# A hybrid decoder step on one core: feed-forward input in a fixed order, cache rows and stores on another queue

## The chip, the cores and the metric

The kernel runs on one core of a Trainium2 chip. The time is device microseconds of one execution, the median of three runs. The engines are named as in the profile: PE (TensorE) with PEld, its weight loads, DVE (VectorE), ACT (ScalarE), POOL (GpSimd) and SP (SyncE). Transfers are issued by SP, POOL and ACT and carried by the core's 16 DMA engines.

## What is computed

One layer of a hybrid causal decoder for 256 prompt tokens and 8 x 4 sample tokens, which share all weights (model width 2048, feed-forward width 5632, everything in float32):

```python
h = _rms_norm(x, g_pre_mix)
(qa, ka, va, za, ba, aa, qb, kb, vb, uc, ga, gb, gc) = _split(h @ w_in, IN_SPLITS)
# A: gated DeltaNet on qa, ka, va -> out_a
# B: dilated sliding-window attention on qb, kb, vb, with the cached windows for the sample tokens -> out_b
# C: multi-scale pooling of uc -> oc
merged = (jax.nn.sigmoid(ga) * (out_a @ w_br_a)
          + jax.nn.sigmoid(gb) * (out_b @ w_br_b)
          + jax.nn.sigmoid(gc) * (oc @ w_br_c))
x = x + _rms_norm(merged @ w_out, g_post_mix)
gate, up = _split(_rms_norm(x, g_pre_ffn) @ w_gu, (D_FF, D_FF))
x = x + _rms_norm((jax.nn.silu(gate) * up) @ w_down, g_post_ffn)
```

Besides the new x, the states are returned: the windows of keys and values (win1, win2, win3), moved on by the new tokens, the DeltaNet state, and the last rows of convolution and pool.

## The kernel before

The 288 tokens are the columns of every activation tile (128 x 288); a weight tile is 256 x 512 values (512 KB) and yields 24 matmuls. Each product is made of three matmuls: weights and activations are split into a rounded part and a rest (wh, wl; xgh, xgl), and wh x xh, wh x xl and wl x xh are added up in PSUM. So each weight tile passes through `feed` (lines 172 to 185): SP loads it into one of five `raw` buffers, ACT casts it to wh (line 180), DVE subtracts to get wl (line 184). Three wh and three wl buffers let this run ahead of PE.

`run_items` goes through a planned list of products. Beside it run generators (`start`, `step`): after every weight tile, each of them emits so many steps as its rate says. The program is not executed in the order in which it is written: a planner puts the instructions of each engine in an order by their simulated times, except where `behind` or `chain` ties one instruction to another. Each engine and each queue then takes its instructions strictly in that order.

**The sample tokens' attention.** `evac_qkv` (line 955 on) copies the new q, k and v out of PSUM, turns them and stores them on POOL's queue (`self.dq`): to the scratch tensor `scr`, and as the newest rows of the output windows (lines 986, 988, 991). `attn_sample` (line 1077 on) is a generator at 4.4 steps a tile. It reads the cached keys, then the cached values, in rows of 128 x 512 values (256 KB) into five buffers `kr` (KR = 5). Of groups 1 and 2 there are 32 + 16 rows for keys and as many for values, loaded on line 1106 from a view whose outermost size is 4 (`src[m, kv][:4]`, then 32 rows of 512 values); of group 0 there are 8 + 8, line 1111, from a view of 128 rows. Rows of the new tokens come from `scr` (lines 1089, 1112). Four rows are fetched ahead (`KR - 1`). Each row of groups 1 and 2 feeds four DVE instructions (lines 1142 for keys, 1192 for values). These are tied to each other and, by `paced`, to the newest wl. The cache copies of line 165 (win_sample<-cache_win) are issued by SP later, from about the middle of the kernel on.

**From the mixer to the feed-forward.** `evac_out` evacuates merged @ w_out block by block: ACT squares it, DVE adds the squares to `nacc`, ACT scales it by g_post_mix into `tt`. After the last block `post_mix` makes one more wh and wl (`feed(3)`) and takes the root of the mean square: `rms_rows` sums over the partitions with small PE matmuls, ACT takes the root, DVE the reciprocal, and PE spreads it over the partitions (rmsb, line 368). `ffn_input` then makes, for each of 16 blocks d, the product of t with rmsb (line 1367), the new x (line 1368), and from it xgh on ACT (line 373) and xgl on DVE (line 374). The first item of the feed-forward is a wide one of 12 tiles that takes the blocks as they come. `ffn_norm` squares the new x and adds the squares up to r2, which the evacuations of the first blocks need (`evac_ffn_gate`).

**The tail.** After the last product `down_done` adds identity x xr into PSUM for the first blocks of kind 'e' in the string TAIL (the x products, line 1433), makes the last `rms_rows`, multiplies every y by it (line 1440) and adds x: 'e' on PE with a copy by ACT, 'q' on POOL, 'v' on DVE (line 1449).

Of the kernel before, what the change touches and what calls it, by code (L numbers as in the profile page):

```python
# [21 lines left out]
TS = 6  # L22
TAIL = 'eveqqqeeeqqqevqe'
PCB = 3
KR = 5
# [63 lines left out]
class Layer:  # L89
# [3 lines left out]
    def __init__(self, ctx, tc, a, o):  # L93
        self.ctx, self.tc, self.nc, self.a, self.o = ctx, tc, tc.nc, a, o
        P = self.pool
        self.cp = P("cp")
        self.raw_p = P("rawp", 5)
        self.wh_p = P("whp", 3)
        self.wl_p = P("wlp", 3)
        self.up = P("up")  # L100
        self.sm = P("sm", 2)
        self.dr = P("dr", space=DRAM)
        self.pm = P("pm", 4, space=PSUM)
        self.pb = P("pb", 4, space=PSUM)
        self.ufree = deque(range(NU))
        self.uslot = {}
        self.bg = []
        self.chained = {}
        self.tiles = deque()
        self.pend = deque()  # L110
        self.items = []
        self.n = 0
        self.paced_to = None
        self.raws = deque()
        self.hold = None
        self.out_a, self.out_b, self.out_c = {}, {}, {}
        self.dq = self.nc.gpsimd
# [54 lines left out]
    def feed(self, ahead):  # L172
        nc = self.nc
        while len(self.pend) < ahead and (self.raws or self.tiles):
            if not self.raws:
                self.load()
            raw = self.raws.popleft()
            wh = self.wh_p.tile([128, 2, 512], F32R, name="wh")
            wl = self.wl_p.tile([128, 2, 512], F32R, name="wl")
            i = nc.scalar.copy(wh, raw)  # L180
            if self.hold is not None:
                self.behind(i, self.hold)
                self.hold = None
            self.last_wl = nc.vector.tensor_tensor(wl, raw, wh.bitcast(F32), op=OP.subtract)  # L184
            self.pend.append((wh, wl))

# [81 lines left out]
    def chain(self, ins, key="sample"):  # L268

        if key in self.chained:  # L270
            self.behind(ins, self.chained[key])
        self.chained[key] = ins

    def paced(self, ins):
# [80 lines left out]
    def rms_rows(self, *accs):  # L355

        nc, st = self.nc, (0, 128, 160)
        p = self.ps("rms")
        for k, acc in enumerate(accs):
            for i, t in enumerate(st):  # L360
                nc.tensor.matmul(p[:, i:i + 1], lhsT=acc[:, t:t + 128], rhs=self.c["ones"][:, 0:1],
                                 start=k == i == 0, stop=k == len(accs) - 1, skip_group_check=True)
        r = self.small(3, "rs")
# [129 lines left out]
    def mixer_plan(self):  # L493
# [53 lines left out]
        for br, off, name, nk in (("a", 9744, "w_br_a", 4), ("c", 13840, "w_br_c", 4), ("b", 11792, "w_br_b", 2)):  # L547
# [8 lines left out]
            for n in range(4):  # L556
                if br == "a" or (br == "c" and n):
# [5 lines left out]
                          after=(lambda br=br: self.branch_done(br)) if n == 3 else None)  # L563
        self.tt, self.xr = {}, {}
        for n in range(4):
# [4 lines left out]
        for part, gs in enumerate(((0, 1, 2), (3, 4, 5), (6, 7, 8), (9, 10))):  # L570
            for f in gs:
                if f == 0:
                    gate, up = self.evac_ffn_gate(0), self.evac_ffn_up(0)
                    self.plan_wide(wg, 8, 0, DFF, lambda: self.xg,
                                   lambda b, ps, gate=gate, up=up: gate(b, ps) if b < 4 else up(b - 4, ps),
                                   ready=lambda t: self.ffn_input(min(16, (t // 3) * 4 + (2, 4, 6)[t % 3])))
                    self.plan_half(wg, 8, DFF + 256, lambda: self.xg, lambda b, ps, up=up: up(b + 2, ps))
                    continue
# [376 lines left out]
    def evac_qkv(self, kind, g):  # L955
        vT = []

        def evac(h, ps):
# [10 lines left out]
            for tb in ([2] if kind == 0 else [1, 2] if (kind == 1 and g == 0) else [0, 1, 2]):  # L969
# [5 lines left out]
                for hp in range(2):  # L975
# [6 lines left out]
                    if tb < 2:  # L982
                        if not (g == 0 and tb == 0):
                            o = self.o[f"win{g + 1}_prompt"][0, 0].rearrange("r k h d -> r k (h d)")
                            r0 = 0 if g == 0 else tb * 128
                            self.dq.dma_start(o[r0:r0 + 128, kind - 1, cs], n[:, :256])
                    else:
                        self.dq.dma_start(self.scr[kind, g][:, cs], n[:NS, :256])
                        if kind > 0:
                            o = self.o[f"win{g + 1}_sample"][0].rearrange("b r k h d -> b r k (h d)")  # L990
                            self.dq.dma_start(o[:, WIN[g] - 4:, kind - 1, cs], n[:NS, :256])
                    if kind == 2 and tb < 2:
# [84 lines left out]
    def attn_sample(self, pool):  # L1077
# [8 lines left out]
        def by_t(dst, kind, g):  # L1086
            src = scr[kind, g].rearrange("(b t) d -> t b d", t=4)
            for t in range(4):
                dq.dma_start(dst[t * 32:t * 32 + 32], src[t][:, None, :].to_broadcast([8, 4, 512]))

# [3 lines left out]
        for t in range(4):  # L1094
            dq.dma_start(big[:, t], q0s[t][:, None, :].to_broadcast([8, 16, 512]))
        cw = [a["cache_win1"][0], a["cache_win2"][0], a["cache_win3"][0]]
# [4 lines left out]
        def sources(kv):  # L1101

            for g, dil, n in ((1, 4, 32), (2, 16, 16)):
                src = cw[g].rearrange("b (q m r) k h d -> m k r (b q) (h d)", q=4, r=dil)
                for m in range(n):
                    yield g, (m if g == 1 else 32 + m), lambda kr, s=src[m, kv][:4]: dq.dma_start(kr, s)  # L1106
            for g in (1, 2):
                yield g, 47 + g, lambda kr, g=g: by_t(kr, 1 + kv, g)
            src = cw[0].rearrange("b (s m) k h d -> m k (b s) (h d)", m=8)
            for m in range(8):  # L1110
                yield 0, m, lambda kr, s=src[m, kv]: dq.dma_start(kr, s)
            yield 0, 8, lambda kr: dq.dma_start(kr, scr[1 + kv, 0][:, None, :].to_broadcast([32, 4, 512]))

# [17 lines left out]

        for _ in range(KR - 1):
            load()
# [204 lines left out]
    def evac_out(self, n):  # L1338
        def evac(b, ps):
# [6 lines left out]
            if k == 9:  # L1346
                self.warm_sqrt(self.nacc)
            t = self.U(name="t")
            nc.scalar.activation(t, ps, AF.Copy, scale=self.p["g_post_mix"][:, k:k + 1])
            self.tt[k] = t  # L1350
        return evac

    def post_mix(self):
        nc = self.nc
        for pr in self.mg.values():
            self.free(*pr)
        self.feed(3)
        self.rmix = self.rms_rows(self.nacc, self.last)
        self.free(self.last)
        self.xg = []  # L1360
        self.ffn_rms = self.start(self.ffn_norm(self.nacc), 1.6)

    def ffn_input(self, n):
        nc = self.nc
        for d in range(len(self.xg), n):
            t, x = self.tt[d], self.xr[d]
            nc.vector.tensor_tensor(t, t, self.rmix, op=OP.mult)
            nc.vector.tensor_tensor(x, x, t, op=OP.add)
            self.xg.append(self.scaled_split(x, self.p["g_pre_ffn"][:, d:d + 1], "xg"))
            self.free(t)  # L1370

    def ffn_norm(self, acc):
        nc = self.nc
        for d in range(16):
            while len(self.xg) <= d:
                yield
            self.sq_add(acc, self.xr[d], d == 0)
            yield
        self.r2 = self.U(name="r2")
        nc.scalar.copy(self.r2, self.rms_rows(acc))  # L1380
        self.free(acc)


    def evac_ffn_gate(self, f):
# [19 lines left out]
    def evac_down(self, part, n):  # L1404
        def evac(b, ps):
# [6 lines left out]
            if part == 3:  # L1412
# [5 lines left out]
                if k == 9:  # L1418
                    self.warm_sqrt(self.nacc)
                nc.scalar.activation(self.y[k], self.y[k], AF.Copy, scale=self.p["g_post_ffn"][:, k:k + 1])  # L1420
        return evac

    def down_done(self, blks, part):
# [3 lines left out]
        if part < 3:  # L1427
            return
        kind = dict(zip(range(16), TAIL))
        pre = {}  # L1430
        for d in [d for d in range(16) if kind[d] == "e"][:TPRE]:
            pre[d] = self.add_bank(len(pre))
            nc.tensor.matmul(pre[d][:, :NT], lhsT=self.c["ident"], rhs=self.xr[d], start=True, stop=False)
        r = self.rms_rows(self.nacc, self.last)
        pool = self.pool("yo", 6)
# [85 lines left out]
```

## Time and profile before

| | us |
|---|---|
| median of 3 runs (2057.72 to 2062.92) | 2061.14 |
| the profiled execution | 2068.37 |
| its span | 2066.6 |
| PE busy in it | 2010.6 |
| mean granted clock | 0.992 |

A row of a table of stages has: its bounds in us from the start, its length; busy us and instructions of PE, PEld, DVE, ACT and POOL; the granted clock; the mean busy share of the 16 DMA engines (over 1 where packets of several queues overlap); and GB/s. A row of a list of transfers has the output and input, the issuing queue, the count, KB each and the median us from issue to landing. A row of DMA queues has packets, MB and the share of the 16 engines' time. A timeline row has start and length in us, engine, line, output<-input, shape, a count where rows in a series were merged, and in brackets the idle time before it with what ended it. A row of waits has the waiting engine with its line, what it waited for, us in total, times, and the longest in us.

### The profile page before, as it was taken

How to read it: one execution, taken by the hardware profiler on the slowest of the kernel's cores; microseconds unless marked ns; L12 is line 12 of the kernel's file. 1: busy time of each engine (PE TensorE's matmuls, PEld its weight loads, DVE VectorE, ACT ScalarE, POOL GpSimd, SP SyncE). 2: the span in 40 equal slices, each digit the busy share in tenths (PEclk: the TensorE clock that was granted, in tenths of full speed). 3: DMA queues.
4: the chain of work that ended last, by engine and by line, in shares of the span. 5: the costliest groups of instructions: out<-in, count | busy, mean ns of one | idle time of the engine just before them, and what ended most of it. 6: DMA issues, size and time to landing. Idle time of an engine off the chain costs nothing. (4 is left out here: it accounts for less than half of the span.)

```text
span 2066.6 us, 38707 instructions
## 1 busy us (share of the span) xinstructions
PE 2010.6 (97%) x15212; PEld 1984.4 (96%) x15212; DVE 1324.2 (64%) x2857; ACT 893.8 (43%) x1414; POOL 291.6 (14%) x504
## 2 busy tenths in 40 slices
PE   8999999999799999989999989999999999999998
PEld 8989998999799999989999989999999999999997
DVE  7969558567688779878875475543554445454555
ACT  6654473453344444333334454334333333333344
POOL 2326312523320022322000000000000000000001
PEclk9999999999999999999999989999999999999999
DMA  8565546959995668998677646766767767677662
GB/s 268 160 182 169 176 140 197 228 173 238 219 205 183 181 184 198 226 220 245 195 229 234 218 160 212 226 222 217 225 216 228 230 217 226 218 225 227 217 205 97
DMA packets 240310, 425.50 MB, mean 206 GB/s; under 512 B 42736, under 2 KB 83200, under 8 KB 238464
## 3 DMA queue, kind: packets, MB, share of 16 engines
q1 hardware_dynamic: 207712, 384.72, 63.1%
q0 software_dynamic: 32272, 37.73, 8.0%
q8 instruction: 119, 1.95, 0.4%
q10 hardware_dynamic: 144, 0.59, 0.1%
q14 instruction: 63, 0.52, 0.1%
HBM read 410.44 MB, written 66.63 MB: 231 GB/s over the span
## 5 line engine op out<-in xcount | busy, mean ns | idle before, releaser
L184 DVE TENSOR_TENSOR wl<-raw,wh 128x1024 fp32r<-128x1024 f32 x585 | 720.2, 1232 | 519.0 <-ACT wh L180 516.7
L180 ACT CAST wh<-raw 128x1024 fp32r<-128x1024 f32 x585 | 612.7, 1050 | 917.9 <-PE m L254 792.3
L253 PE MATMUL m<-hh,wh 128*128 128x288 f32 x1792 | 532.7, 299 | 4.2 <-ACT wh L180 3.7
L255 PE MATMUL m<-hh,wl 128*128 128x288 f32 x1792 | 524.0, 298 | 8.3 <-DVE wl L184 8.3
L254 PE MATMUL m<-hl,wh 128*128 128x288 f32 x1792 | 531.3, 298 | 0.0
L253 PE MATMUL m<-xgh,wh 128*128 128x288 f32 x1408 | 415.8, 297 | 4.0 <-ACT xgh L373 4.0
L254 PE MATMUL m<-xgl,wh 128*128 128x288 f32 x1408 | 415.8, 296 | 3.2 <-DVE xgl L374 3.2
L255 PE MATMUL m<-xgh,wl 128*128 128x288 f32 x1408 | 414.6, 296 | 0.0
L255 PEld LDWEIGHTS m<-hh,wl 128*128 128x128 f32 x1792 | 335.1, 189 | 13.1 <-DVE wl L184 10.7
L253 PEld LDWEIGHTS m<-hh,wh 128*128 128x128 f32 x1792 | 337.7, 189 | 7.8 <-ACT wh L180 4.2
L254 PEld LDWEIGHTS m<-hl,wh 128*128 128x128 f32 x1792 | 338.2, 189 | 1.9 <-issue 1.8
L253 PEld LDWEIGHTS m<-xgh,wh 128*128 128x128 f32 x1408 | 265.5, 189 | 4.6 <-ACT xgh L373 4.3
L254 PEld LDWEIGHTS m<-xgl,wh 128*128 128x128 f32 x1408 | 266.4, 189 | 3.6 <-DVE xgl L374 3.5
L255 PEld LDWEIGHTS m<-xgh,wl 128*128 128x128 f32 x1408 | 265.4, 189 | 0.0
L253 PE MATMUL m<-hidh,wh 128*128 128x288 f32 x704 | 207.5, 295 | 0.0
L254 PE MATMUL m<-hidl,wh 128*128 128x288 f32 x704 | 207.2, 295 | 0.0
L255 PE MATMUL m<-hidh,wl 128*128 128x288 f32 x704 | 206.5, 295 | 0.0
L1449 POOL TENSOR_TENSOR yo<-y,xr 128x288 f32<-128x288 f32 x7 | 5.6, 821 | 1060.7 <-DVE y L1440 1060.7
L254 PEld LDWEIGHTS m<-hidl,wh 128*128 128x128 f32 x704 | 132.4, 188 | 0.0
L253 PEld LDWEIGHTS m<-hidh,wh 128*128 128x128 f32 x704 | 132.2, 188 | 0.0
L255 PEld LDWEIGHTS m<-hidh,wl 128*128 128x128 f32 x704 | 131.9, 188 | 0.0
L1106 POOL DMA_DIRECT2D kr<-cache_win x96 | 65.4, 682 | 250.0 <-DVE junk L1142 136.9
(386 smaller groups left out, 2704.4 us busy)
## 6 DMA issues: line engine op xcount, KB each, us to landing
raw<-w_in SPq DMA_DIRECT2D x247, 512.0 KB, 4.5
raw<-w_gu SPq DMA_DIRECT2D x176, 512.0 KB, 4.0
raw<-w_down SPq DMA_DIRECT2D x88, 512.0 KB, 4.9
win_sample<-cache_win SPq DMA_DIRECT2D x64, 512.0 KB, 5.4
kr<-cache_win POOLq DMA_DIRECT2D x112, 256.0 KB, 10.7
raw<-w_out SPq DMA_DIRECT2D x32, 512.0 KB, 5.0
win_sample<-cache_win SPq DMA_DIRECT2D x32, 508.0 KB, 5.2
st<-state_gdn SPq DMA_DIRECT2D x64, 128.0 KB, 3.2
```

The source lines that it names most:

```text
L180: i = nc.scalar.copy(wh, raw)
L184: self.last_wl = nc.vector.tensor_tensor(wl, raw, wh.bitcast(F32), op=OP.subtract)
L253: nc.tensor.matmul(out, lhsT=wh[:, c], rhs=xh, start=k == 0, stop=False)
L254: nc.tensor.matmul(out, lhsT=wh[:, c], rhs=xl, start=False, stop=False)
L255: nc.tensor.matmul(out, lhsT=wl[:, c], rhs=xh, start=False, stop=k == nk - 1)
L1106: yield g, (m if g == 1 else 32 + m), lambda kr, s=src[m, kv][:4]: dq.dma_start(kr, s)
L1449: (nc.vector if how == "v" else nc.gpsimd).tensor_tensor(out[:, d % 2], y, x, op=OP.add)
```

## The change

- In `evac_qkv` and `attn_sample`, the stores of the new rows, the loads from `scr` and all loads of cache rows are issued by SP instead of POOL, and three rows instead of four are fetched ahead (`KR - 2`).
- `ffn_input` ties product, sum and rest into one DVE chain: for the blocks of one call first product and sum of each, then the rests. The first wl after it is tied behind its last sum (`hold_wl`). `post_mix` no longer feeds. The squares in `ffn_norm` are added behind the newest wl, at 1.1 steps a tile instead of 1.6.
- The first feed-forward blocks are copied out of PSUM as they are; product with r2, SiLU and split follow in the generator `ffn_first`.
- The scaling of the last four blocks, of t and of y, comes after the last square.
- `rms_rows` is cut into `rms_sums` and `rms_bcast`; in the tail the x products are tied behind the sums. Two blocks of kind 'v' become 'e'.

```diff
-TAIL = 'eveqqqeeeqqqevqe'
+TAIL = 'eeeqqqeeeqqqeeqe'
...
             self.last_wl = nc.vector.tensor_tensor(wl, raw, wh.bitcast(F32), op=OP.subtract)
+            if self.hold_wl is not None:
+                self.behind(self.last_wl, self.hold_wl)
+                self.hold_wl = None
...
     def rms_rows(self, *accs):
 
+        return self.rms_bcast(self.rms_sums(*accs)[0])
+
+    def rms_sums(self, *accs):
...
+        return p, m
+
+    def rms_bcast(self, p):
+        nc, st = self.nc, (0, 128, 160)
...
                 if f == 0:
-                    gate, up = self.evac_ffn_gate(0), self.evac_ffn_up(0)
-                    self.plan_wide(wg, 8, 0, DFF, lambda: self.xg,
-                                   lambda b, ps, gate=gate, up=up: gate(b, ps) if b < 4 else up(b - 4, ps),
+                    self.first = []
+                    self.plan_wide(wg, 8, 0, DFF, lambda: self.xg, self.evac_ffn_first,
                                    ready=lambda t: self.ffn_input(min(16, (t // 3) * 4 + (2, 4, 6)[t % 3])))
-                    self.plan_half(wg, 8, DFF + 256, lambda: self.xg, lambda b, ps, up=up: up(b + 2, ps))
+                    self.plan_half(wg, 8, DFF + 256, lambda: self.xg, self.evac_ffn_first,
+                                   after=lambda: self.start(self.ffn_first(), 1))
...
-                            self.dq.dma_start(o[r0:r0 + 128, kind - 1, cs], n[:, :256])
+                            nc.sync.dma_start(o[r0:r0 + 128, kind - 1, cs], n[:, :256])
...
-                        self.dq.dma_start(self.scr[kind, g][:, cs], n[:NS, :256])
+                        nc.sync.dma_start(self.scr[kind, g][:, cs], n[:NS, :256])
...
-                            self.dq.dma_start(o[:, WIN[g] - 4:, kind - 1, cs], n[:NS, :256])
+                            nc.sync.dma_start(o[:, WIN[g] - 4:, kind - 1, cs], n[:NS, :256])
...
-                dq.dma_start(dst[t * 32:t * 32 + 32], src[t][:, None, :].to_broadcast([8, 4, 512]))
+                nc.sync.dma_start(dst[t * 32:t * 32 + 32], src[t][:, None, :].to_broadcast([8, 4, 512]))
...
-                    yield g, (m if g == 1 else 32 + m), lambda kr, s=src[m, kv][:4]: dq.dma_start(kr, s)
+                    yield g, (m if g == 1 else 32 + m), lambda kr, s=src[m, kv][:4]: nc.sync.dma_start(kr, s)
...
-                yield 0, m, lambda kr, s=src[m, kv]: dq.dma_start(kr, s)
-            yield 0, 8, lambda kr: dq.dma_start(kr, scr[1 + kv, 0][:, None, :].to_broadcast([32, 4, 512]))
+                yield 0, m, lambda kr, s=src[m, kv]: nc.sync.dma_start(kr, s)
+            yield 0, 8, lambda kr: nc.sync.dma_start(kr, scr[1 + kv, 0][:, None, :].to_broadcast([32, 4, 512]))
...
-        for _ in range(KR - 1):
+        for _ in range(KR - 2):
             load()
...
-            t = self.U(name="t")
-            nc.scalar.activation(t, ps, AF.Copy, scale=self.p["g_post_mix"][:, k:k + 1])
-            self.tt[k] = t
+            self.todo.append((k, ps))
+            for k, ps in (self.todo if k < 12 or k == 15 else ()):
+                self.tt[k] = self.U(name="t")
+                nc.scalar.activation(self.tt[k], ps, AF.Copy, scale=self.p["g_post_mix"][:, k:k + 1])
+            if k < 12 or k == 15:
+                self.todo = []
...
-        self.feed(3)
...
-        self.ffn_rms = self.start(self.ffn_norm(self.nacc), 1.6)
+        self.ffn_rms = self.start(self.ffn_norm(self.nacc), 1.1)
...
-        for d in range(len(self.xg), n):
+        ds = range(len(self.xg), n)
+        for d in ds:
             t, x = self.tt[d], self.xr[d]
-            nc.vector.tensor_tensor(t, t, self.rmix, op=OP.mult)
-            nc.vector.tensor_tensor(x, x, t, op=OP.add)
-            self.xg.append(self.scaled_split(x, self.p["g_pre_ffn"][:, d:d + 1], "xg"))
+            self.chain(nc.vector.tensor_tensor(t, t, self.rmix, op=OP.mult), "xg")
+            self.hold_wl = self.chain(nc.vector.tensor_tensor(x, x, t, op=OP.add), "xg")
             self.free(t)
+            hi = self.U(dt=F32R, name="xgh")
+            nc.scalar.activation(hi, x, AF.Copy, scale=self.p["g_pre_ffn"][:, d:d + 1])
+            self.xg.append((hi, self.U(dt=F32R, name="xgl")))
+        for d in ds:
+            hi, lo = self.xg[d]
+            self.chain(nc.vector.scalar_tensor_tensor(lo, self.xr[d], self.p["g_pre_ffn"][:, d:d + 1], hi.bitcast(F32),
+                                                      op0=OP.mult, op1=OP.subtract), "xg")
...
+                nc.scalar.activation(t, self.xr[d], AF.Square)
+                self.behind(nc.vector.tensor_tensor(acc, acc, t, op=OP.add), self.last_wl)
...
+    def evac_ffn_first(self, b, ps):
+        t = self.U(name="ff")
+        self.nc.scalar.copy(t, ps)
+        self.first.append(t)
+
+    def ffn_first(self):
+
+        nc = self.nc
+        self.drain(self.ffn_rms)
+        for b in range(4):
+            t, u = self.first[b], self.first[4 + b]
+            nc.vector.tensor_tensor(t, t, self.r2, op=OP.mult)
+            nc.scalar.activation(t, t, AF.Silu)
+            nc.vector.tensor_tensor(u, u, self.r2, op=OP.mult)
+            nc.vector.tensor_tensor(t, t, u, op=OP.mult)
+            self.hid[b] = self.split(t, "hid")
+            self.free(t, u)
+            yield
...
-                nc.scalar.activation(self.y[k], self.y[k], AF.Copy, scale=self.p["g_post_ffn"][:, k:k + 1])
+                for j in ([k] if k < 12 else range(12, 16) if k == 15 else ()):
+                    nc.scalar.activation(self.y[j], self.y[j], AF.Copy, scale=self.p["g_post_ffn"][:, j:j + 1])
...
+        sums, prev = self.rms_sums(self.nacc, self.last)
         pre = {}
         for d in [d for d in range(16) if kind[d] == "e"][:TPRE]:
             pre[d] = self.add_bank(len(pre))
-            nc.tensor.matmul(pre[d][:, :NT], lhsT=self.c["ident"], rhs=self.xr[d], start=True, stop=False)
-        r = self.rms_rows(self.nacc, self.last)
+            prev = self.behind(nc.tensor.matmul(pre[d][:, :NT], lhsT=self.c["ident"], rhs=self.xr[d], start=True,
+                                                stop=False), prev)
+        r = self.rms_bcast(sums)
```

More of the change, by code (lines that the diff above doesn't have):

```diff
@@ L114, in __init__ @@
         self.raws = deque()
-        self.hold = None
+        self.hold = self.hold_wl = None
         self.out_a, self.out_b, self.out_c = {}, {}, {}
@@ L272, in chain @@
         self.chained[key] = ins
+        return ins
     def paced(self, ins):
@@ L360, in rms_rows @@
             for i, t in enumerate(st):
-                nc.tensor.matmul(p[:, i:i + 1], lhsT=acc[:, t:t + 128], rhs=self.c["ones"][:, 0:1],
-                                 start=k == i == 0, stop=k == len(accs) - 1, skip_group_check=True)
+                m = nc.tensor.matmul(p[:, i:i + 1], lhsT=acc[:, t:t + 128], rhs=self.c["ones"][:, 0:1],
+                                     start=k == i == 0, stop=k == len(accs) - 1, skip_group_check=True)
+        return p, m
+    def rms_bcast(self, p):
+        nc, st = self.nc, (0, 128, 160)
         r = self.small(3, "rs")
@@ L563, in mixer_plan @@
                           after=(lambda br=br: self.branch_done(br)) if n == 3 else None)
-        self.tt, self.xr = {}, {}
+        self.tt, self.xr, self.todo = {}, {}, []
         for n in range(4):
@@ L1094, in attn_sample @@
         for t in range(4):
-            dq.dma_start(big[:, t], q0s[t][:, None, :].to_broadcast([8, 16, 512]))
+            nc.sync.dma_start(big[:, t], q0s[t][:, None, :].to_broadcast([8, 16, 512]))
         cw = [a["cache_win1"][0], a["cache_win2"][0], a["cache_win3"][0]]
@@ L1376, in ffn_norm @@
                 yield
-            self.sq_add(acc, self.xr[d], d == 0)
+            if d == 0:
+                nc.scalar.activation(acc, self.xr[d], AF.Square)
+            else:
+                t = self.U(name="sq")
+                nc.scalar.activation(t, self.xr[d], AF.Square)
+                self.behind(nc.vector.tensor_tensor(acc, acc, t, op=OP.add), self.last_wl)
+                self.free(t)
             yield
```

## The prediction

> **What bounds the kernel now.** First the busy times of the page, then the table of stages, to find where TensorE loses time.
>
> ```profile
> span 2066.6 us, 38707 instructions
> PE 2010.6 (97%) x15212; PEld 1984.4 (96%) x15212; DVE 1324.2 (64%) x2857; ACT 893.8 (43%) x1414; POOL 291.6 (14%) x504
> ...
> 455.00:607.00 152.00, 138.97 (x1031) 136.85 (x1030) 110.04 (x422) 62.26 (x97) 45.49 (x73) 0.98 0.99 217
> 772.00:933.00 161.00, 150.49 (x1103) 147.88 (x1102) 134.10 (x282) 60.18 (x77) 44.60 (x68) 0.99 1.00 217
> 1300.00:1400.00 100.00, 100.00 (x757) 100.00 (x756) 49.34 (x60) 39.49 (x50) 0.00 (x0) 1.00 0.71 225
> 1193.31:1212.28 18.97, 10.05 (x49) 9.16 (x48) 16.93 (x44) 12.66 (x32) 0.00 (x0) 0.64 0.19 56
> 1242.00:1244.00 2.00, 2.00 (x17) 2.00 (x17) 0.84 (x2) 0.21 (x1) 0.00 (x0) 1.00 1.06 412
> ```
>
> TensorE is the bound: in a plain stretch (1300 to 1400) it never rests and starts 757 matmuls in 100 us, 0.132 us each, 3.17 us for a weight tile of 24. It loses time in three places that the change touches. In the two stretches in which attn_sample reads cache rows PE is idle 152.00 - 138.97 = 13.0 us and 161.00 - 150.49 = 10.5 us, and there alone the DMA share (last but one column) is about 1.0 at only 217 GB/s. Between the mixer and the feed-forward it spends 18.97 us on what is otherwise some 4 us of work. The third is the tail.
>
> Now what is moved in the two row stretches, the first four lines from 455 to 607, the others from 772 to 933 (count, KB each, median us from issue to landing):
>
> ```profile
> raw<-w_in SPq DMA_DIRECT2D x35, 512.0 KB, 10.2
> kr<-cache_win POOLq DMA_DIRECT2D x43, 256.0 KB, 10.1
> raw<-w_br_a SPq DMA_DIRECT2D x4, 512.0 KB, 9.2
> win_prompt<-nat POOLq DMA_DIRECT2D x14, 128.0 KB, 9.2
> ...
> raw<-w_in SPq DMA_DIRECT2D x29, 512.0 KB, 11.1
> kr<-cache_win POOLq DMA_DIRECT2D x43, 256.0 KB, 12.8
> raw<-w_br_c SPq DMA_DIRECT2D x15, 512.0 KB, 11.4
> raw<-w_pool SPq DMA_DIRECT2D x4, 256.0 KB, 4.6
> ```
>
> Each stretch holds 43 rows (line 1106) beside 39 or 46 weight tiles' worth, and everything lands late. The rows of line 1106 are no ordinary transfers. Two of them when hardly anything else runs on POOL's queue, first one of line 1111 (656 to 668), then one of line 1106 (696 to 707):
>
> ```profile
> q0 software_dynamic: 80, 0.26, 7.1%
> kr<-cache_win POOLq DMA_DIRECT2D x1, 256.0 KB, 3.2
> ...
> q0 software_dynamic: 272, 0.26, 9.7%
> kr<-cache_win POOLq DMA_DIRECT2D x1, 256.0 KB, 6.8
> ```
>
> Same queue, same 256 KB, but 6.8 us to landing instead of 3.2 and 272 packets instead of 80. The 192 extra ones carry next to nothing (0.26 MB both times), and 192 = 12 x 16. The difference in the code is the outermost size of the source: `[:4]` on line 1106, 128 rows on line 1111. I read a line 1106 row as **narrow**: four of the 16 DMA engines carry it.
>
> **The change part by part.**
>
> *Rows and stores to SyncE.* Removed from POOL are 43 + 43 narrow rows in these stretches and the small stores; SP issues them between the weight loads, in one queue, in order. What a narrow row costs on SP's queue no row shows: all its transfers now are wide. By the stage table the engines reach 412 GB/s at a share of 1.06, so 389 GB/s in all, 24.3 GB/s each. A weight tile puts 32 KB on each engine, 1.35 us. Spread over all 16, a row would put 16 KB there, 0.67 us; on four, 64 KB, 2.70 us. Bounds: below, rows that spread, or whose four engines move on from row to row, so that no engine is full and the idle 13.0 + 10.5 = 23.5 us can vanish; above, a narrow row that holds the queue as long as it did alone, 6.8 less the 3.2 - 0.67 that a wide row needs beside its data, 4.3 us. I take 2.70 us on the same four engines each time, the value that the nearest row, the narrow one alone, gives by its shape: a weight tile is complete only when these four have done their part of it too.
>
> Then these four have, in the first stretch, 43 x 2.70 + 39 x 1.35 + 14 x 0.34 (the 128 KB stores) = 116.1 + 52.7 + 4.8 = 173.6 us to do in 152.0: +21.6. In the second 116.1 + 46 x 1.35 = 178.2 in 161.0: +17.2. The idle times of before are inside the 152 and 161, so nothing is to be taken off for them. What was fetched ahead, three rows (KR - 2), needn't be waited for at the start: 8.1 us off once (in the second stretch the wide transfers I didn't count stand against it). **Sum +31 us.** DVE doesn't hide this: a row feeds four of its operations at 4.4 operations a tile, and every next wl stands behind them (paced).
>
> The waits that SP gains: a row waits for the row two before to be used up, a store for the copy on ACT or DVE, and behind each stand weight loads.
>
> ```profile
> SPq L169 <- DVE junk L1142: 134.0, 36, 9.8
> ACT oah L146 <- DMA win_sample<-nat: 17.9, 2, 9.2
> PE pv L1065 <- ACT pT L1057: 6.8, 1, 6.8
> ```
>
> SP waits for buffers anyway, 134.0 us between 450 and 620, and five raw buffers are some 15 us of TensorE's work, so a wait of 2 or 3 us there costs nothing by itself. What goes: ACT was held twice for some 9 us because a store behind waiting rows on POOL landed late, and PE stood 6.8 us behind that. On SP the store stands behind weight loads and rows that wait likewise; I count no gain beyond the stage sums.
>
> The Trainium skill has the rule for which engines (page "DMA: Bandwidth & Descriptors", section "Why a DMA increments its semaphore by 16 and not by 1"): the number of engines is the largest up to 16 that divides the outermost sizes of both sides; from GpSimd the group then moves on by a round-robin cursor, from SP it is always the lowest-numbered ones. By it the sum is the +31 above; that the group stays the same on SP no run here shows.
>
> *Feed-forward input, block by block.*
>
> ```profile
> 1195.41 1.23 DVE L184 TENSOR_TENSOR wl<-raw,wh 128x1024 fp32r<-128x1024 f32 x1 [1.30 <-ACT wh L180]
> 1195.76 0.26 ACT L364 ACTIVATE rs<-rms,eps 128x3 f32<-128x3 f32 x1 [0.39 <-PE rms L361]
> 1196.55 0.17 DVE L365 RECIPROCAL rs<-rs 128x3 f32<-128x3 f32 x1
> 1197.35 3.00 DVE L1367 TENSOR_TENSOR t<-t,rmsb 128x288 f32<-128x288 f32 x8 [0.63 <-PE rmsb L368]
> 1200.28 0.45 DVE L1368 TENSOR_TENSOR xr<-xr,t 128x288 f32<-128x288 f32 x1
> 1200.76 0.54 ACT L373 ACTIVATE xgh<-xr,sp 128x288 fp32r<-128x288 f32 x1 [4.74 <-DVE xr L1368]
> 1201.35 1.81 PE L253 MATMUL m<-xgh,wh 128*128 128x288 f32 x6 [4.03 <-ACT xgh L373]
> 1205.78 0.51 DVE L374 SCALAR_TENSOR_TENSOR xgl<-xr,sp,xgh 128x288 fp32r<-128x288 f32 x1
> 1206.34 0.61 PE L254 MATMUL m<-xgl,wh 128*128 128x288 f32 x1 [3.19 <-DVE xgl L374]
> 1206.34:1212.28 5.94, 5.94 (x25) 5.94 (x26) 5.94 (x16) 5.94 (x17) 0.00 (x0) 0.50 0.00 0
> ```
>
> DVE does eight products before the first sum, and the first xgl comes last of all: PE goes on at 1206.34, 9 us after rmsb. In the chained order product (0.37 us from start to start: eight in 3.00), sum (0.45), xgh on ACT (0.54) and xgl (0.51) follow one another: 1.9 us, with the steps between engines some 2.2 us after rmsb. rmsb comes some 0.4 us sooner: rs is there at 1196.02, and the wl (1.23) that holds the reciprocal until 1196.55 is now made after the first two blocks. So PE goes on at about 1197.0 + 2.2 = 1199.2 instead of 1206.34; the six matmuls of 1201.35 are to be taken off, 0.8 us. That leaves 6.3 us. After the stop the clock is at 0.50 and 25 matmuls take 5.94 us instead of 3.3: 2.6 us lost, that may stay or go; I leave it. Against it stands DVE from there on: 16 x (0.37 + 0.37 + 0.43) + 12 wl x 1.15 + 16 square adds x 0.37 = 38.4 us (durations of the rows less the 0.08 us by which the next one starts early) beside 12 tiles x 3.17 = 38.0 us: it has no room, and I take 0.8 us for tiles that come late. The first block's evacuation as copies adds 8 ACT copies beside an ACT that is 39% busy, and the products with r2 only later: nothing, as PE waits for no bank there now. **Sum -5.5 us**, between -9 (clock and all) and +1 (the order costs as much as it gives, and a wl of 1.15 stands in front).
>
> *Tail.*
>
> ```profile
> 2050.00 2.10 PE L1433 MATMUL yo<-xr,cc 128*128 128x288 f32 x8
> 2051.94 0.72 PE L361 MATMUL rms<-cc,nacc 128*128 128x1 f32 x6
> 2053.90 0.54 PE L368 MATMUL rmsb<-cc,rs 128*128 128x128 f32 x3 [0.56 <-DVE rs L365]
> 2054.48 4.82 DVE L1440 TENSOR_TENSOR y<-y,rmsb 128x288 f32<-128x288 f32 x13 [0.64 <-PE rmsb L368]
> 2059.22 1.05 DVE L1449 TENSOR_TENSOR yo<-y,xr 128x288 f32<-128x288 f32 x1
> ```
>
> The sums can start 0.7 us before 2051.94 (the last square ends near 2051.1), but the five x products (0.52 us each) then stand between them and rmsb: 2.6 us where 1.2 us is free. Two adds of DVE (1.05) become PE work of about the same length. **-0.5 us**, from -2 to +1.
>
> Together +31 - 5.5 - 0.5 = +25. The profiled execution took 2068.4 us (span 2066.6), so it would take 2093; against the median of 2061.1 it is **2086 us**.
>
> **The rivals.** (1) *The rows spread on SP's queue* (the other side: faster). If the engines of successive rows change, the fullest has 43 x 0.67 + 53 = 82 us in 152, PE sets the pace and idles no more: -23.5 at most, -12 if half the idle time has other causes (DVE is 134.10 of 161.00 busy). With -6 elsewhere: 2043, between 2031 and 2050. It decides at a row price of (152.0 - 57.5) / 43 = 2.2 us: below it the first stretch gets no longer. For it: POOL's own rows, 43 in 152 us, would fill a fixed group of four by 116 us before any weights, and yet the mean share of all is 0.99, so they move about there. Against it: that is another queue. (2) *The queue doesn't matter*: the same bytes on the same engines, -6 alone, 2055. The skill's page has that rule too (section "Issuing engines are not separate DMA queues": DMAs of all issuers interleave on the same 16 engines). (3) *A narrow row costs more than 2.70 us*: at 3.2 us, +21.5 per stretch, 2129. (4) *The order doesn't hold on DVE*, since only the x chain is fixed and wl and squares may be put between: the 5.5 us don't come, 2091.
>
> **How the numbers follow.** Forecast with (4) beside it 0.50 (2070 to 2110); (1) 0.30; (2) 0.12, half of it within 0.3% of 2061; (3) 0.08. 0.3% (6 us) is about what a measurement of this kernel can tell from no change. Slower: 0.48 of the forecast and (3), 0.56; same: 0.02 of the forecast and 0.06, 0.08; faster: 0.30 + 0.06 = 0.36. The range goes from the middle of (1) to a bit over the forecast's own: 2036 to 2112.
>
> **What would show it.** Right: narrow rows landing late on SP's queue, DVE's longest waits for kr and ACT's for raw, PE idle 30 us or more in each row stretch, the DMA share well below 1 there, as twelve engines wait for four. Wrong: PE busy throughout both stretches, rows landing in 4 to 6 us. For the feed-forward: the first xgl some 2 us after rmsb and PE's wait under 3 us; for the tail rmsb before 2053.9 less what the rest shifts. The forecast is wrong if the group of engines changes from row to row, and its size if the rate of an engine isn't 24.3 GB/s.

## The result, and the profile after

| | before | after |
|---|---|---|
| median of 4 runs, us | 2062.03 (2057.72 to 2064.61) | 2144.85 (2142.10 to 2147.89) |
| span of the profiled execution, us | 2066.6 | 2146.1 |

The ratio of after to before is 1.040, 95% interval 1.038 to 1.043: slower by 83 us where 25 were forecast, and outside the range. First the page of the changed kernel, then its table of stages (columns as before: PE busy stands after the length; the last three are PE clock, DMA share, GB/s).

```profile
span 2146.1 us, 38710 instructions
PE 2034.8 (95%) x15220; PEld 2000.0 (93%) x15220; DVE 1323.5 (62%) x2855; ACT 895.4 (42%) x1424; POOL 170.7 (8%) x312
```
```profile
500.00:550.00 50.00, 40.49 (x272) 38.79 (x270) 26.42 (x106) 14.93 (x24) 0.00 (x0) 0.92 0.57 173
550.00:600.00 50.00, 34.82 (x234) 33.70 (x235) 25.78 (x98) 13.61 (x22) 0.00 (x0) 0.83 0.56 167
600.00:650.00 50.00, 40.30 (x282) 39.69 (x282) 33.21 (x124) 19.93 (x33) 0.00 (x0) 0.86 0.57 171
900.00:950.00 50.00, 37.23 (x243) 35.11 (x242) 29.13 (x58) 11.71 (x14) 3.27 (x4) 0.90 0.54 159
950.00:1000.00 50.00, 36.07 (x242) 34.00 (x242) 28.00 (x60) 11.71 (x14) 3.23 (x4) 0.93 0.58 175
```

PE starts 234 to 282 matmuls in 50 us, where a full stretch has some 378, and the DMA engines are not full: share 0.57, where it was about 1.0 before. Neither side is busy, so something between them is. The list of transfers, in 40 slices of half a microsecond from 960 to 980 (busy tenths of the 16 engines, then GB/s), shows what:

```profile
DMA  2579962222222223989962222248998422278896
GB/s 86 143 205 348 340 197 78 82 98 98 98 98 86 98 98 106 164 229 340 250 168 86 94 86 98 98 147 221 307 315 188 119 94 94 102 147 221 311 373 143
```

Long plateaus at 2 tenths and 98 GB/s are four engines at 24.5 GB/s, carrying one row; the short peaks at 9 are weight tiles on all 16. They take turns. SP's own list says the same (start, length of the issue, which was 0.37 us for a weight tile before):

```profile
570.09 3.13 SPq L1117 DMA_DIRECT2D kr<-cache_win  x2
573.32 2.57 SPq L169 DMA_DIRECT2D raw<-w_in  x1
575.98 1.18 SPq L1117 DMA_DIRECT2D kr<-cache_win  x1
577.24 2.87 SPq L169 DMA_DIRECT2D raw<-w_in  x1
580.21 1.26 SPq L1117 DMA_DIRECT2D kr<-cache_win  x1
```

Each line starts 0.1 us after the end of the one before, so SP stands at no semaphore between them: the issue itself is slow. I read that as a queue that is full; the trace doesn't show the queue's filling. And so the engines wait (us in all, times, longest; 450 to 1050):

```profile
ACT wh L180 <- DMA raw<-w_in: 94.5, 32, 7.5
...
DVE ot L1203 <- DMA kr<-cache_win: 49.4, 29, 5.0
...
DVE junk L1153 <- DMA kr<-cache_win: 48.1, 25, 3.5
...
ACT oah L146 <- DMA win_sample<-nat: 29.3, 2, 16.2
```

DVE's waits for rows were 21.8 and 15.0 us before, ACT's for w_in tiles 17.7.

To see where the time came in, I paired the 585 wl instructions of both traces in order and took the difference of their starts. It has grown by 8.6 us when the first rows have been fetched ahead (by 1.0 before the first row), by 39 in the first row stretch, by 37 in the second, falls by 6.4 at the feed-forward input, drifts by -1.5 and -0.6 in between, and the tail adds 2.7: 79.5 us, the difference of the spans (0.5 more between the stretches). **The fetching ahead and the two row stretches make up 84 of it**, with the stores in them. Of the 79.5 us, 24.2 stand as longer busy time of PE (2034.8 - 2010.6) for the same matmuls but eight: where PE stops the clock is lower, 0.83 in the worst 50 us.

### The profile page after: what moved, and what is told of

It reads as the page before. It is cut to its first block, busy times and chain, and to the rows that moved or that the text cites. A ratio compares the mean times of both kernels' runs of the same rounds, so it can differ in the third digit from the quotient of the medians.

```text
span 2146.1 us, 38710 instructions
## 1 busy us (share of the span) xinstructions
PE 2034.8 (95%) x15220; PEld 2000.0 (93%) x15220; DVE 1323.5 (62%) x2855; ACT 895.4 (42%) x1424; POOL 170.7 (8%) x312
## 5 line engine op out<-in xcount | busy, mean ns | idle before, releaser
L258 PE MATMUL m<-hh,wl 128*128 128x288 f32 x1792 | 530.2, 301 | 26.8 <-DVE wl L184 26.8
L256 PE MATMUL m<-xgh,wh 128*128 128x288 f32 x1408 | 410.0, 296 | 3.1 <-ACT xgh L1385 3.0
L258 PEld LDWEIGHTS m<-hh,wl 128*128 128x128 f32 x1792 | 339.4, 191 | 34.4 <-DVE wl L184 32.2
L256 PEld LDWEIGHTS m<-hh,wh 128*128 128x128 f32 x1792 | 342.2, 191 | 16.9 <-ACT wh L180 11.2
L257 PEld LDWEIGHTS m<-hl,wh 128*128 128x128 f32 x1792 | 342.6, 191 | 2.6 <-issue 2.5
L1203 DVE SCALAR_TENSOR_TENSOR ot<-kr,sct,ot 128x128 f32<-128x128 f32 x196 | 70.3, 359 | 53.5 <-DMA kr<-cache_win 49.4
```

The lines of the kernel that those rows point to most:

```text
L256: nc.tensor.matmul(out, lhsT=wh[:, c], rhs=xh, start=k == 0, stop=False)
L257: nc.tensor.matmul(out, lhsT=wh[:, c], rhs=xl, start=False, stop=False)
L258: nc.tensor.matmul(out, lhsT=wl[:, c], rhs=xh, start=False, stop=k == nk - 1)
L1203: self.paced(e.scalar_tensor_tensor(dst, kr[:, hs], pr, dst, op0=OP.mult, op1=OP.add))
```

## The experiments

All kernels start from the changed one unless said otherwise. Ratios are to the kernel before, with 95% intervals. It took 2063 to 2067 us beside the different sets of runs, so a difference of times between e1 to e4, e5 to e9, e10 to e13, e14 to e16 and e17 is uncertain by a few us.

### Which part of the change

e1_no_queue_move undoes the whole queue move:

```diff
-                            nc.sync.dma_start(o[r0:r0 + 128, kind - 1, cs], n[:, :256])
+                            self.dq.dma_start(o[r0:r0 + 128, kind - 1, cs], n[:, :256])
...
-                    yield g, (m if g == 1 else 32 + m), lambda kr, s=src[m, kv][:4]: nc.sync.dma_start(kr, s)
+                    yield g, (m if g == 1 else 32 + m), lambda kr, s=src[m, kv][:4]: dq.dma_start(kr, s)
...
-        for _ in range(KR - 2):
+        for _ in range(KR - 1):
```

> The changed kernel with every row, scr load and store issued by POOL again, and KR - 1 rows ahead; the feed-forward and tail parts stay. All theories agree that the loss sits in the queue move. By the alignment of the traces the feed-forward input gives 6, the tail costs 3, the rest drifts by 1.5: 2062 - 6 + 3 - 1.5 = about 2057, between 2053 and 2062. Above 2075 the order of the feed-forward or of the tail would be a cause as well, and the queue move a smaller one.

Measured 2059.13 us, 0.998 (0.996 to 1.000). All of the loss sits in the queue move.

e2_rows_on_sp_only undoes only the first kind of line (the three stores), e3_stores_on_sp_only all the others.

> The changed kernel with the three stores of evac_qkv (win_prompt, scr, win_sample) on POOL again; rows and scr loads stay on SP. Theory A (narrow rows: each holds the same four engines, and the next weight load waits behind it): most of the +85 us stays, 2120 to 2140. Theory B (the stores on SP wait for the copies and hold the weight loads, some 15 us each time): the loss goes down to the predicted sum, 2075 to 2095.

> The changed kernel with rows and scr loads on POOL again (KR - 1 ahead) and only the stores on SP. Theory A: no narrow transfer is on SP, so the time is that without a queue move, 2053 to 2063. Theory B: the stores' waits hold the weight loads here too, 2080 to 2105.

Measured 2138.04 (1.036; 1.033 to 1.039) and 2057.01 us (0.997; 0.995 to 0.999). The stores alone cost nothing on SP; the rows alone cost all but 7 us. In e3 the order of instructions on DVE and PE is the changed kernel's, one for one, so the 88 us between e3 and the changed kernel come from the queue of the rows and scr loads and from one row of lead less.

### Is it the shape of the row?

e4_rows_spread issues a narrow row as four transfers, whose outermost size is 32 instead of 4:

```diff
+        def by_r(kr, s):
+            for r in range(4):
+                nc.sync.dma_start(kr[r * 32:r * 32 + 32], s[r])
...
-                    yield g, (m if g == 1 else 32 + m), lambda kr, s=src[m, kv][:4]: nc.sync.dma_start(kr, s)
+                    yield g, (m if g == 1 else 32 + m), lambda kr, s=src[m, kv][:4]: by_r(kr, s)
```

> The changed kernel, in which each narrow row (128 partitions, outermost size of the source 4) is issued as four transfers of 32 partitions with outermost size 32, all on SP as before; bytes, waits and place in the queue stay. Theory A: the rows spread over the engines, a row costs 0.67 us of each instead of 2.70 of four, and the row stretches lose nothing any more: 2050 to 2070. Theory B: the stores and the waits in SP's order are still there, 2090 or more. If what costs is the number of SP's issues, four times as many make it worse than 2145.

Measured 2044.33 us, 0.990 (0.987 to 0.993): 100.5 us less than the changed kernel, with the same bytes, queue and order on DVE and PE, and four times as many issues. Its table of stages, the same 50 us as above:

```profile
500.00:550.00 50.00, 42.83 (x322) 42.06 (x321) 32.87 (x125) 16.38 (x25) 0.00 (x0) 1.00 0.75 221
550.00:600.00 50.00, 50.00 (x367) 49.41 (x366) 41.98 (x156) 26.03 (x42) 0.00 (x0) 0.97 0.86 249
900.00:950.00 50.00, 50.00 (x383) 50.00 (x381) 45.93 (x93) 18.27 (x20) 5.61 (x8) 1.00 0.83 261
```

PE never rests in the second stretch, at 261 GB/s instead of 159. In the first 7 us are still lost, where the stores stand. e5_rows_spread_stores_pool puts these back on POOL (the edit of e2):

> The spread rows of e4_rows_spread on SP, with the three stores of evac_qkv on POOL again. With narrow rows, taking the stores off SP gave 2145 - 2138 = 7 us. If the stores' waits on SP are a cost of their own, it comes here too: 2035 to 2041, and TensorE's idle 7 us between 500 and 550 goes. If they only cost where the narrow rows stand behind them, no change: 2042 to 2047.

Measured 2034.64 us, 0.985 (0.982 to 0.987), the fastest with e13 below, and faster than both the kernel before and the changed one. Its first stretch has no idle PE:

```profile
500.00:550.00 50.00, 50.00 (x384) 49.90 (x383) 41.47 (x158) 23.14 (x37) 8.67 (x16) 1.00 0.89 262
```

So the stores cost 7 to 10 us where rows stand in the same queue (14 between e9 and e10 below, by the ratios 12), and nothing without them.

e8_rows_two_engines makes the row narrower: two transfers, each with outermost size 2 (`kr[r * 32:r * 32 + 64]` from `s[r:r + 2]`, r = 0 and 2).

> The changed kernel, with each narrow row as two transfers whose outermost size is 2, both on SP. Theory A (a transfer of k parts goes to the k lowest engines, each time the same ones): two engines carry a row, 5.4 us of each at 24.3 GB/s, so a row stretch takes 43 x 5.4 + 57 = 290 us and more, where it is 190 now: at least 100 us longer each, 2330 or more in all. If the second transfer of a row goes to two other engines, the load stays that of four: 2130 to 2160.

Measured 2360.32 us, 1.142 (1.138 to 1.147). Its GB/s from 560 to 580, and SP's list from 574:

```profile
GB/s 49 47 49 49 33 31 49 53 143 221 393 287 275 287 283 225 78 49 45 49 49 49 49 41 49 49 49 49 49 49 135 176 299 385 148 53 45 49 49 49
```
```profile
574.68 4.17 SPq L1106 DMA_DIRECT2D kr<-cache_win  x2
...
581.47 3.93 SPq L1106 DMA_DIRECT2D kr<-cache_win  x2
...
595.31 3.80 SPq L1106 DMA_DIRECT2D kr<-cache_win  x2
```

49 GB/s: two engines, and the second transfer of a row isn't carried beside the first by two others, or the plateau would stand at 98. Three rounds of a row and a weight tile take 595.31 - 574.68 = 20.63 us, 6.88 each; less 1.35 for the weight tile a row costs 5.5 us. The same from SP's list of e2_rows_on_sp_only:

```profile
566.64 1.17 SPq L1117 DMA_DIRECT2D kr<-cache_win  x1
...
570.96 1.25 SPq L1117 DMA_DIRECT2D kr<-cache_win  x1
...
575.24 1.29 SPq L1117 DMA_DIRECT2D kr<-cache_win  x1
```

4.30 us a round, 2.95 a row: twice the engines, half the price. This price halves and doubles with the number of engines, as it would if the same ones carry every row. A queue that finished one transfer before the next would show the same; on ACT's queue e11 below tells the two apart.

### Is it SP's queue, or the engines?

e6_no_queue_move_spread is e1 with the spread rows on POOL.

> No queue move (rows, scr loads and stores on POOL, KR - 1 ahead), but each narrow row as four transfers that spread. Theory C: the shape of the transfer is what costs, on either queue, and SP gains nothing of its own: 2040 to 2050, as e4_rows_spread. Theory D: on POOL the group of engines moves from row to row anyway, so that spreading gains nothing there and the gain of e4_rows_spread is due to SP's queue: 2055 to 2065, as without the spreading.

Measured 2102.23 us, 1.017 (1.015 to 1.020), and neither theory. The planner put PE's and DVE's instructions in a much more different order here than in the kernels above, and 42 us are one wait, behind the last values:

```profile
PE so L1215 <- DVE big L1207: 42.0, 1, 42.0
```

That is as much as the difference from e1 (43 us). The rows themselves land after 2.9 us instead of 9.2 (median, 500 to 600 here, where each transfer is a quarter of a row, 450 to 650 in e1), but what spreading is worth on POOL stays open.

e11_narrow_on_act lets ACT issue the narrow rows (`nc.scalar.dma_start`; the rest as in e2), so that no weight load is queued behind them; e12_spread_on_act does that with spread rows.

> The narrow rows as they are, but issued by ACT, so that no weight load stands behind one in its queue; the other rows stay on SP, the stores on POOL. To be read against e12_spread_on_act, since ACT's own waits for free row buffers may cost something in both. Theory L (the four lowest engines carry a narrow row whoever of the two issues it, and every weight load needs them too): slower than e12_spread_on_act by 40 us or more. Theory Q (a narrow row is dear only as it stands in the weight loads' own queue and holds SP): within 15 us of e12_spread_on_act.

> The control of e11_narrow_on_act: the narrow rows as four spread transfers each, issued by ACT. If ACT's issues and waits cost nothing, 2035 to 2045 as with spread rows on SP; what is above that is the price of issuing on ACT, in both kernels.

Measured 2122.85 us (1.029; 1.027 to 1.032) and 2061.34 (0.999; 0.997 to 1.000). The 61 us between them are no measure of the engines' load alone: the planner's order differs in a tenth of DVE's instructions, and ACT, which casts the weights, is itself held by its issues of narrow rows, up to 3.9 us each. SP's issues of weight tiles keep their 0.37 us in e11 (460 to 650), and ACT's waits for w_in tiles (450 to 1050) are 20.3 us, against 94.5 in the changed kernel; DVE's for rows 110.7, against 97.5. What e11 does show is which engines carry a row. Its trace from 560 to 580 has the known plateau:

```profile
GB/s 180 274 401 275 94 111 115 102 102 98 102 98 102 98 102 98 98 139 176 332 344 221 172 262 344 250 131 98 102 127 209 340 385 189 98 98 102 98 98 102
```

Below are two issues of rows on ACT, neither held up, and the queues from 563 to 563.7, from 563.7 to 565.4 and from 565.6 to 568.5 (q1 is SP's with the weights, q10 ACT's with the rows; the last number is the share of the 16 engines' time):

```profile
562.63 0.54 ACTq L1117 DMA_DIRECT2D kr<-cache_win  x1
...
563.98 0.54 ACTq L1117 DMA_DIRECT2D kr<-cache_win  x1
...
q1 hardware_dynamic: 23, 0.05, 17.7%
q10 hardware_dynamic: 16, 0.03, 12.2%
...
q10 hardware_dynamic: 43, 0.09, 13.1%
q1 hardware_dynamic: 43, 0.09, 13.1%
...
q10 hardware_dynamic: 146, 0.29, 26.2%
```

At first the end of a weight tile and a row take turns on four to five engines; from 565.6 on the rows alone have four, 26.2% of 16, though by the count of their packets only 28 of the 32 rows issued were done at 563.98. The 28th row ends at 563.7 and the next begins at once, and still the tile's end and the new row have two engines' time each. Had the new row gone to four other engines, it would have had all four of these, and the tile's end the four that came free. So on ACT's queue successive rows have the same four engines, and it is on these four that the weight tile's end is late. That SP's queue does the same is inferred from the rates.

In e12 ACT waits 91.4 us for its own spread rows to land, and the planner's order differs from e5's in a seventh of DVE's instructions; how much of the 27 us above e5 (2061 against 2035) each of them makes was not tried.

### From which load on does it cost?

e9_half_spread spreads only every second row (`by_r(kr, s) if m % 2 else nc.sync.dma_start(kr, s)`); e10_half_spread_stores_pool has the stores on POOL as well.

> The changed kernel with every second narrow row spread. Theory A1 (the load of the fullest engines against TensorE's time decides): a row costs (3.1 + 0.67) / 2 = 1.9 us of the four engines on the mean, under the 2.2 us from which a stretch gets longer, so nearly nothing is lost: 2044 to 2060. Theory A2 (each narrow row holds the weight loads behind it by itself, whatever slack there is): half of the loss stays, some 2095.

> Every second narrow row spread, as in e9_half_spread, and the three stores of evac_qkv on POOL, as in e5_rows_spread_stores_pool (2035) and e2_rows_on_sp_only (2138, all rows narrow). Theory A1 (a stretch gets longer only from a mean row price on; with a narrow row and the weight load behind it at 4.3 us of SP's queue and a spread one at some 2.75, 43 rows take 151 us of the 152): nearly all of the gain is there once the stores are gone, 2035 to 2060. Theory A2 (each narrow row costs its own time, whatever slack there is): half of the 103 us between the two, some 2086.

Measured 2087.32 (1.010; 1.007 to 1.013) and 2073.36 us (1.005; 1.003 to 1.006): 43 of 101 and 39 of 103 us of the loss remain. That looks like a price for each row, but there is lead as a rival. Hence six row buffers (`KR = 6`), in e2 (e14_narrow_six_rows) and in e10 (e15_half_spread_six_rows):

> e2_rows_on_sp_only (2138: all rows narrow on SP, stores on POOL) with six row buffers instead of five, so four rows of lead instead of three. Load (a narrow row and the weight load behind it take 4.3 us of the queue, 43 of them 185 us where TensorE needs some 150): the lead only helps at the start of a stretch, by one row each, 2128 to 2138. Lead (the rows come late since they are asked for late): a good part of the loss goes, 2110 or less.

> e10_half_spread_stores_pool (2073: every second row spread, stores on POOL) with six row buffers. The queue has room here (43 rows at a mean of some 3.5 us, 151 us). Lead: DVE's waits for rows go for the most part, 2040 to 2058. Load: 2068 to 2073.

Measured 2125.75 (1.030; 1.027 to 1.033) and 2064.61 us (1.000; 0.998 to 1.001), 12 and 9 us less. In e14 the waits move rather than vanish (450 to 1050):

```profile
ACT wh L180 <- DMA raw<-w_in: 123.8, 40, 7.4
...
DVE junk L1153 <- DMA kr<-cache_win: 31.3, 24, 3.3
...
DVE ot L1203 <- DMA kr<-cache_win: 20.0, 14, 3.0
```

In e2 they were 105.0, 70.1 and 46.8: rows come earlier, weights later. With all rows narrow, load decides far more than lead. In e15 SP itself waits for narrow rows to land:

```profile
SPq L169 <- DMA kr<-cache_win: 58.3, 24, 3.6
```

That wait is made by the experiment: in the program's list SP's transfers use eight semaphores in turn, so that each waits for the eighth before it, and rows of four transfers use these up. So the half-spread kernels can't answer the question. e17_half_on_pool halves the narrow rows on SP without splitting any (from e2):

```diff
-                    yield g, (m if g == 1 else 32 + m), lambda kr, s=src[m, kv][:4]: nc.sync.dma_start(kr, s)
+                    yield g, (m if g == 1 else 32 + m), lambda kr, q=dq if m % 2 else nc.sync, s=src[m, kv][:4]: q.dma_start(kr, s)
```

> e2_rows_on_sp_only (2138: all narrow rows on SP, stores on POOL) with every second narrow row issued by POOL instead, whole, with nothing split; the order on DVE and PE is that of e2 to a few lines. With all narrow rows on POOL it took 2057 to 2059. Load (the four engines have 21.5 x 3.1 + 21.5 x 0.67 + 53 = 134 us to do in a stretch of 152): nearly all of the loss goes, 2050 to 2070. A price for each narrow row on SP whatever slack there is: half of the loss stays, some 2098.

Measured 2080.62 us, 1.009 (1.007 to 1.011): 22 of the 79 us between e1 and e2 remain, between the two theories. Half the rows cost well under half, so it is no price for each row; but a good deal is lost below the limit too.

### The feed-forward input and the tail

e13_spread_stores_pool_tail_old is e5 with the tail of before:

```diff
-TAIL = 'eeeqqqeeeqqqeeqe'
+TAIL = 'eveqqqeeeqqqevqe'
...
-        sums, prev = self.rms_sums(self.nacc, self.last)
...
-        r = self.rms_bcast(sums)
+        r = self.rms_rows(self.nacc, self.last)
```

e16_before_rows_spread is the kernel before with spread rows and scr loads on SP, stores on POOL and three rows of lead: e13 without the feed-forward part.

> The spread rows on SP with the stores on POOL (2035), and the tail as it was before the change. By the alignment of the traces the changed tail costs 2.7 us: 2030 to 2034. By the predicted step (the tail gains 0.5): 2035 to 2036. The two are hardly told apart by the time, but by the trace: from the last wl to the end of the span 3 us less, or not.

> The kernel before, with rows and scr loads on SP, each narrow row as four spread transfers, the lead of three rows, and the stores left on POOL: that is e13_spread_stores_pool_tail_old (2034) without the feed-forward part. If that part gives what the traces of before and after show, 5 to 6.5 us: 2039 to 2041. If the order doesn't hold on DVE, no difference: 2032 to 2036.

Measured 2034.13 (0.986; 0.985 to 0.988) and 2039.47 us (0.988; 0.986 to 0.990). The feed-forward part is worth 5.3 us (4 by the ratios), though the intervals overlap. The tail makes no difference that can be measured, and the miss was mine: the expected 2.7 us came from a profile in which the tail fell on a low clock. Tail rows of the changed kernel, then of e3_stores_on_sp_only, with the same tail:

```profile
2129.37 4.26 PE L1480 MATMUL yo<-xr,cc 128*128 128x288 f32 x10
...
2129.84 0.18 DVE L376 RECIPROCAL rs<-rs 128x3 f32<-128x3 f32 x1 [1.99 <-ACT rs L375]
...
2133.46 0.49 PE L379 MATMUL rmsb<-cc,rs 128*128 128x128 f32 x3
```
```profile
2037.87 2.67 PE L1480 MATMUL yo<-xr,cc 128*128 128x288 f32 x10
...
2038.34 0.18 DVE L376 RECIPROCAL rs<-rs 128x3 f32<-128x3 f32 x1 [1.89 <-ACT rs L375]
...
2040.38 0.49 PE L379 MATMUL rmsb<-cc,rs 128*128 128x128 f32 x3
```

The same x products take 4.26 and 2.67 us; from 2129 to 2131 the granted clock is 0.54, in e3 from 2038 to 2040.4 it is 1.00. rmsb waits for them 3.4 us after the reciprocal in the one, 1.9 in the other.

## Why the prediction was right in direction and wrong in size

**Narrow rows on the same four engines: right.** 98 GB/s on the plateaus is 24.5 GB/s an engine (assumed 24.3), 49 with two. The prediction named a rule of the Trainium skill ("DMA: Bandwidth & Descriptors", section "Why a DMA increments its semaphore by 16 and not by 1") and left open whether the group stays the same on SP. The runs now agree with that rule: 5.5 us for two engines and 2.95 for four is the price of a group that stays, on ACT's queue the trace shows it stay (e11), and the same rows on POOL cost nothing of the kind (e1). Which of the 16 engines they are no record tells.

**The step that failed is the term of +31 for rows and stores on SP: it was mis-sized and measured 84.** Its parts:

- *The row at 2.70 us* is 2.95 in the steady rounds: 43 x 0.25 = 11 us in each stretch. Four engines are busy in every slice, so these 0.25 us aren't a stop; where they go stays open.
- *The waits of SP at nothing* was wrong as soon as the rows are there: the stores cost 7 us (e2) to 10 us (e5). "A wait of 2 or 3 us there costs nothing by itself" holds only for e3, where the queue has room.
- *The 8.1 us off for rows fetched ahead* had the wrong sign; they cost 7.6 (8.6 less the 1.0 from before the first row). Five narrow rows stood in front of five weight tiles, and SP was held from 393.94 to 414.60:

```profile
393.94 9.63 SPq L1117 DMA_DIRECT2D kr<-cache_win  x5
403.69 10.91 SPq L169 DMA_DIRECT2D raw<-w_in  x5
```

- *Nothing for the clock.* 24 us of the 79.5 appear as slower matmuls after stops. A stretch bound by its transfers could hide some of that; how much of it is a cost by itself was not tried.

Together the first stretch grew by 39 us (forecast 21.6) and the second by 37 (17.2). In the first, 21.6 + 11 + 7 for the stores come to that, with nothing left for the clock; in the second 17.2 + 11 leave 9 us open. Rival (3), a row price of 3.2 us and 2129, was the nearest of the cases named.

**The limit of 2.2 us is not sharp.** Rival (1) said that below this mean price a stretch gets no longer. At a mean near 1.8 (half of the rows at 2.95, half at 0.67) e17 still lost 22 of 79 us. Rows and weights come in turns, and a DVE that is 84 to 92% busy where PE never rests (e4) makes up no late row; that is argued, not shown.

**Rival (1), spread rows on SP: did not happen, but its time was right.** Made to spread (e4), the kernel takes 2044, forecast 2043. That it fits so well is luck: the rival took half of the 23.5 us of idle time as staying and the stores as free, while e5 (2035) shows nearly all of it go and the stores take some 10 us back.

**Feed-forward -5.5: right.** -6.4 in the paired traces of before and after (6.4 to 6.5 in the traces of e2, e5 and e17, paired with that of before in the same way), 4 to 5.3 in the runs. In the trace of after the chain holds as drawn, and rival (4) is out: the first xgl comes 2.6 us after the start of rmsb, and the wl stands behind it.

```profile
1280.13 0.54 PE L379 MATMUL rmsb<-cc,rs 128*128 128x128 f32 x3 [0.56 <-DVE rs L376]
1280.71 0.45 DVE L1381 TENSOR_TENSOR t<-t,rmsb 128x288 f32<-128x288 f32 x1 [0.63 <-PE rmsb L379]
1281.19 0.46 DVE L1382 TENSOR_TENSOR xr<-xr,t 128x288 f32<-128x288 f32 x1
...
1282.73 0.52 DVE L1389 SCALAR_TENSOR_TENSOR xgl<-xr,sp,xgh 128x288 fp32r<-128x288 f32 x1
1283.17 1.22 DVE L184 TENSOR_TENSOR wl<-raw,wh 128x1024 fp32r<-128x1024 f32 x1
```

**Tail -0.5: wrong in the profile shown (+2.7), nothing that the runs can tell.** The five x products do stand between the sums and rmsb, as the step had it; it did not reckon with PE stopping for the last squares before the sums, after which the clock may be low just there.

## What to carry to other kernels

Before a transfer is moved to another queue, ask how many DMA engines its outermost size gives it and whether that queue moves on from engine to engine: a transfer on few engines that costs little on one queue can hold up everything on another. A DMA share of 0.57 with PE idle was the mark of it here, and plateaus of GB/s in the slices told the number of engines. Cutting the transfer so that it spreads took 100 us off, and with the small stores left on POOL the move became a gain of 1.2% by itself (e16), 1.5% with the feed-forward part (e5).

## What the runs showed of the hardware that was not expected

- A narrow transfer makes the issue of the next one slow: SP's issue of a weight tile goes from 0.37 us to 2.57 and 2.87 in the rows above, although nothing is waited for between the issues. It belongs to the queue: with the rows on ACT (e11, 460 to 650) SP's issues stay at 0.37 us, and ACT's issues of rows go from 0.54 up to 3.7.
- On ACT's queue, too, narrow rows are carried by four engines, by the same four from row to row: with several rows on their way the share is 26.2% of 16 (e11).
- After a stop of about 1 us PE ran the same ten matmuls in 2.67 us in some profiles and 4.26 in others, at granted clocks of 1.00 and 0.54. What decides it was not tried.
